# HGRN scores on four column strips, one input block on ScalarE's queue, a norm weight on GpSimd, and new figures for the planner

## The chip, the cores and the metric

The kernel runs on one core of a Trainium2 chip, as one program in one launch. The metric is device time in microseconds (us), from the first instruction to the end of the last, and a program's time is the median of its runs. The core's engines are TensorE (PE; its weight loads PEld), VectorE (DVE), ScalarE (ACT), GpSimd (POOL) and SyncE (SP), which here only issues transfers (DMAs). Each engine works through a queue of its own in order, and they wait for one another by semaphores. SBUF is the working memory; PSUM holds what PE writes.

## What is computed

One layer over 512 frames of width 2048. All is float32.

```python
proj = einsum('btd,dc->btc', x, w_in)              # 2048 -> 8320 columns
rw   = token_shift(proj[..., :4224])               # y + mu * (y one frame earlier - y)
r, k, v, z, wd, ad = split(rw)
# RWKV-7, 16 heads of 64: a gated recurrence over frames
kk = k * k_k;  kk = kk / max(norm(kk per head), 1e-12)
S_t = S_(t-1) * decay_t + (S_(t-1) a_t) b_t + v_t k_t;   o_t = S_t r_t
o_rwkv = (group_norm(o) + sum(r * k * r_k) * v) * silu(z)
# HGRN2, 8 heads of 128: gated linear recurrence, over chunks of 64 frames
att[t, s] = sum_d q[t, d] exp(b[t, d] - b[s, d]) k[s, d]   for s <= t
o_hgrn = rms_norm(att i + state part) * g_norm_w * silu(z)
y   = concat(o_rwkv, o_hgrn) @ w_out
out = layer_norm(ALPHA * x + y) * ln_w + ln_b
```

## The kernel before

*The main stream.* Nearly all of PE's work is the two projections. Each float32 operand is split in a high part of type fp32r (`xh`, `wh`) and the rest (`xl`, `wl`), and `three` (L485) issues high x high, high x low and low x high: three main matmuls of 128x128 by 128x512 for one block. Weights arrive in 512 KB tiles `wr` (two of them), on SP's queue, and each half tile is a *part*: `split` takes its high part on ScalarE (`wh`, L361) and the rest on VectorE (`wl`, L371). A part feeds 12 main matmuls. The input units come in a fixed order (`_order`), k, r, v, z for a pair of RWKV heads, then q, f, i, g for the HGRN heads; results are taken out of PSUM by queued evacuations (`shift`, `silu2`, `gates`: L362 on ScalarE, then L380 on VectorE).

*The planner.* Everything else is written as generators of `Op`s, which wait in queues: `preps` (`rwkv_prep`), `turns` (`rwkv_turn`), `groups`, `scans`, `heads` (`hgrn_heads`), `ends` (`hgrn_out`) and more. After each main matmul `plan.pump()` looks at the head of every queue and issues what it thinks can start. It keeps a clock for each engine, and each `Op` has a price in us for each engine that could do it; where there are two (`copy`: ScalarE or VectorE) the one that ends earlier is taken. A PE instruction is put in only when its operands, by these clocks, are nearly there. So the prices issue nothing, but they set the order of the instructions on all five engines. On the chip the engines follow that order and wait where it was too early. `SETS` lists in which function tables of ScalarE a function is found; the planner adds 1.3 to an `Op` whose table isn't the one it thinks loaded. The table loads themselves (ACT_TABLE_LOAD) are put in later, where the order needs them.

*What the steps of the prediction touch.*
- `turned` transposes a tile in 32x32 blocks on VectorE (`dtr`, L390), writes it to DRAM (`far<-q` for the `bk` tile of an RWKV pair, `far<-ksq` for others) and loads it back by rows (`q<-far`, four loads), all on SP's queue (L327). It tells the planner when the loads will have landed: 4.0 after the issue.
- `rwkv_prep` makes head norms: squares, `head_sums` (VectorE adds two halves, ScalarE takes the high part, VectorE the rest, into `ksq`), a product with a block of ones on PE (`mix<-ksq,ones_r`, L348), then Ln and Exp on ScalarE. `rwkv_turn` calls `turned` for `bk`, copies the turned tile on ScalarE (`q<-q`, 128x1024), and makes a second product with `ones_r`. So there are 8 copies and 16 such products.
- `hgrn_heads` builds a head's 128x128 score blocks from products of blocks of 32, 64 and smaller, of two heads at a time. At width 64 it makes both the scores between neighbours of 32 (`w1` = 32) and of 64 (`w1` = 64) in one bank of PSUM, and copies them into the block-diagonal tiles `dgs`. A product is placed in PSUM at a partition offset `g`: products with another offset stand on another strip of PE's columns.
- `fetch` loads the 16 input blocks `head[k]` (512 columns of x and three weight blocks). Block 0 comes in three pieces, one on ScalarE's queue; blocks 1 to 15 come whole, on SP's. `arrive` splits them. Before the first product PE runs nine products of zeros (L1225); the first three units are made by `product` (L1275).
- `row_last` and `finish_last` make the last 128 rows' last 512 columns, in two halves: add, statistics (L1632), the layer norm's mean and reciprocal root (`spread`, with the root on GpSimd, L403), products with the norm's weight (`less_mean`, `weigh`), two products on PE that bring the bias in (`made`), and the last four multiply-adds and stores.

## Time and profile before

| | |
|---|---|
| median of 3 runs | 1031.55 us (1031.42 to 1031.56) |
| the profiled execution's own time | 1033.02 us |
| its span, first instruction to last | 1031.2 us |
| PE busy | 1020.1 us, 99% |
| DVE, ACT, POOL busy | 789.9, 478.4, 42.6 us |
| granted clock | 1.00 |
| DMA | 130.82 MB, 127 GB/s in the mean |

A profile's page gives the busy time of each engine, the chain of work that ended last, and groups of equal instructions with their count, mean duration and the idle time before them. A timeline row has the start and the duration in us, engine, line, operation, out<-in tiles, shapes and a count; in brackets stands how long the engine had been idle and what released it. Main matmuls overlap in the pipeline: a row shows about 0.39 us for one, but their starts are what counts. A float32 product that isn't fp32r leaves two records. Lines are those of the kernel before.

### The profile page before, as it was taken

What the parts mean: (1) busy time and instruction counts of PE and PEld (TensorE: products, weight loads), DVE (VectorE), ACT (ScalarE), POOL (GpSimd) and SP (SyncE); (2) the same over time, 40 slices, a digit from 0 to 9 for tenths busy, and PEclk for the clock granted to TensorE, in tenths of its full rate; (3) what the DMA queues carried; (4) which work ended last, traced back from release to release, by engine and by line L of the source; (5) the groups of instructions that cost most, each with busy time, mean ns of one, the idle gap of its engine ahead of it and who ended that gap; (6) DMA issues with size and microseconds to landing.
All of it is one profiled execution on the core that took longest, in us unless ns stands there. A gap on an engine that the chain in (4) does not pass through costs nothing.

```text
span 1031.2 us, 19527 instructions
## 1 busy us (share of the span) xinstructions
PE 1020.1 (99%) x7636; PEld 843.2 (82%) x7636; DVE 789.9 (77%) x1687; ACT 478.4 (46%) x898; POOL 42.6 (4%) x77
## 2 busy tenths in 40 slices
PE   9999999999999999999999999999999999999997
PEld 8888878888878888888887888887888888888885
DVE  7477997679779988698998758887998888526556
ACT  6457344545363356464534554636435544323321
POOL 0000001001000010020000100100001010000000
PEclk9999999999999999999999999999999999999999
DMA  9134442233635322345353243253432256435613
GB/s 337 53 104 127 138 125 88 78 103 113 183 105 157 122 73 81 92 138 183 105 152 105 82 114 118 92 172 111 147 106 81 63 175 226 149 117 172 200 55 133
DMA packets 58700, 130.82 MB, mean 127 GB/s; under 512 B 9840, under 2 KB 25712, under 8 KB 58480
## 3 DMA queue, kind: packets, MB, share of 16 engines
q1 hardware_dynamic: 58464, 129.37, 39.7%
q8 instruction: 60, 0.98, 0.4%
q14 instruction: 32, 0.26, 0.1%
q10 hardware_dynamic: 144, 0.20, 0.1%
HBM read 111.06 MB, written 18.48 MB: 126 GB/s over the span
## 4 chain that ended last, share of the span: by engine, by line
PE 94%; DMA 2%; DVE 2%; ACT 1%; issue 1%; SPq 0%; DVEq 0%; ACTq 0%
PE main L485 71%; PE mix L348 9%; PE mix L485 8%; PE main L1275 3%; PE main L348 2%; DMA q<-far 1%; DMA far<-q 1%; PE mix L1225 0%; DVE inv L380 0%; SPq L327 0%; DVE wl L371 0%; DVE big L371 0%; DVE q L413 0%; DVE big L390 0%; ACT wh L361 0%
## 5 line engine op out<-in xcount | busy, mean ns | idle before, releaser
L485 PE MATMUL main<-xh,wl 128*128 128x512 f32 x864 | 340.0, 393 | 0.0
L485 PE MATMUL main<-xh,wh 128*128 128x512 f32 x864 | 339.5, 393 | 0.0
L485 PE MATMUL main<-xl,wh 128*128 128x512 f32 x864 | 339.0, 392 | 0.0
L361 ACT ACTIVATE wh<-wr 128x512 fp32r<-128x512 f32 x299 | 185.7, 626 | 194.4 <-PE main L485 139.0
L371 DVE TENSOR_TENSOR wl<-wr,wh 128x512 fp32r<-128x512 f32 x299 | 203.6, 682 | 56.0 <-ACT wh L361 53.9
L485 PEld LDWEIGHTS main<-xh,wh 128*128 128x128 f32 x864 | 162.4, 188 | 33.1
L485 PEld LDWEIGHTS main<-xh,wl 128*128 128x128 f32 x864 | 162.3, 188 | 33.1
L485 PEld LDWEIGHTS main<-xl,wh 128*128 128x128 f32 x864 | 162.3, 188 | 33.0
L485 PE MATMUL main<-wh,xl 128*128 128x512 f32 (+1 forms) x262 | 102.4, 391 | 0.0
L485 PE MATMUL main<-wh,xh 128*128 128x512 f32 (+1 forms) x262 | 101.8, 389 | 0.5 <-ACT t L362 0.5
L485 PE MATMUL main<-wl,xh 128*128 128x512 f32 (+1 forms) x262 | 101.9, 389 | 0.0
L485 PEld LDWEIGHTS main<-wh,xh 128*128 128x128 f32 x262 | 49.2, 188 | 10.8 <-ACT t L362 1.0
L485 PEld LDWEIGHTS main<-wh,xl 128*128 128x128 f32 x262 | 49.2, 188 | 10.0
L485 PEld LDWEIGHTS main<-wl,xh 128*128 128x128 f32 x262 | 49.2, 188 | 9.9
L362 ACT ACTIVATE t<-main,om 128x512 f32<-128x512 f32 x33 | 22.3, 686 | 51.9 <-PE main L485 42.6
L380 DVE SCALAR_TENSOR_TENSOR bd<-mix,pc,bd 64x64 f32<-64x64 f32 x112 | 31.7, 283 | 11.6 <-PE mix L348 7.8
L371 DVE TENSOR_TENSOR inv<-inv,inv 64x30 f32<-64x30 f32 (+14 forms) x120 | 38.5, 321 | 2.7
L371 DVE TENSOR_TENSOR inv<-inv 64x30 f32<-64x30 f32 (+14 forms) x120 | 38.5, 321 | 2.5
L380 DVE SCALAR_TENSOR_TENSOR t<-main,pr,t 128x511 f32<-128x511 f32 x33 | 24.3, 745 | 19.6 <-ACT t L362 19.5
L361 ACT ACTIVATE t<-mix 64x128 f32<-64x128 f32 (+2 forms) x66 | 18.0, 276 | 44.3 <-DVE zz L371 23.5
L371 DVE TENSOR_TENSOR t<-t,tot 128x256 f32<-128x256 f32 x96 | 37.2, 418 | 0.2
L362 ACT ACTIVATE t<-main 128x512 f32<-128x512 f32 x32 | 18.6, 593 | 28.7 <-PE main L485 28.6
(228 smaller groups left out, 1408.1 us busy)
## 6 DMA issues: line engine op xcount, KB each, us to landing
wr<-w_all SPq DMA_DIRECT2D x156, 512.0 KB, 3.6
q<-head SPq DMA_DIRECT2D x15, 448.0 KB, 5.8
far<-ksq SPq DMA_DIRECT2D x22, 256.0 KB, 3.2
far<-q SPq DMA_DIRECT2D x8, 512.0 KB, 5.0
q<-far SPq DMA_DIRECT2D x32, 128.0 KB, 4.4
g<-x_r SPq DMA_DIRECT2D x16, 256.0 KB, 4.0
t<-far SPq DMA_DIRECT2D x56, 64.0 KB, 3.5
spill<-g SPq DMA_DIRECT2D x12, 256.0 KB, 2.8
```

Of the source, the lines that this page charges most:

```text
L348: return Op([("pe", cost, lambda: pe.matmul(o, l, r, start=start, stop=stop, **kw))], [l, r], [o], mode="narrow" if narrow else "main" if ...
L361: return "act", cost, lambda: sc_e.activation(o, i, f, scale=scale)
L362: return "act", cost, lambda: sc_e.activation(o, i, f, scale=scale, bias=bias)
L371: return dve_op([a, b], o, lambda: dve.tensor_tensor(o, a, b, f), base=0.16 if o.shape[0] < P and size(o) == C and o.tensor.name in tags e ...
L380: return dve_op([a, b], o, lambda: dve.scalar_tensor_tensor(o, a, s, b, f1, f2), per=0.00113, base=0.085 if o.shape[0] == P else 0.25 if s ...
L485: pe.matmul(ps, l, r, start=first and i == 0, stop=last and i == 2)
L1275: pe.matmul(pss[a], *ops, start=k == 0 and low == of == 0, stop=k == KT - 1 and low == 1)
```

## The change

`hgrn_heads` puts the products of blocks of 32 on four strips of partitions in turn, where they stood on two, and copies them out in four pieces a head, where there were two. `fetch` issues block 1 on ScalarE's queue. In the last half row the multiply with the norm's weight goes to GpSimd, and is issued ahead of the statistics' root; it no longer stands in `finish_last`. The other edits change the planner's figures: Exp is found in its own table alone; `turned` tells 4.2, and 5.2 for 128x1024, as the time to landing; `tensor_scalar` and `copy` on VectorE are priced by whether they read PSUM; small `scalar_tensor_tensor`s, and transposes of 128 partitions, have new prices. `head_sums` passes a base price of 0.15.

```diff
--- before.py
+++ after.py
@@ -57,7 +57,7 @@
     return o + [(2, 14), (2, 15), (3, 13), (3, 14), (3, 15)]
 
 
-SETS = {AF.Sigmoid: ("sigmoid",), AF.Tanh: ("exp", "sigmoid"), AF.Exp: ("exp", "ln"), AF.Ln: ("ln",)}
+SETS = {AF.Sigmoid: ("sigmoid",), AF.Tanh: ("exp", "sigmoid"), AF.Exp: ("exp",), AF.Ln: ("ln",)}
 
 
 class Plan:
@@ -367,18 +367,23 @@
     def dve_op(reads, o, f, n=None, per=0.00104, base=0.07):
         return Op([("dve", base + (n or size(o)) * per, f)], reads, [o])
 
-    def tt(o, a, b, f=ALU.mult):
+    def tt(o, a, b, f=ALU.mult, base=None):
         return dve_op([a, b], o, lambda: dve.tensor_tensor(o, a, b, f),
-                      base=0.16 if o.shape[0] < P and size(o) == C and o.tensor.name in tags else 0.07)
+                      base=base or 0.16 if o.shape[0] < P and size(o) == C and o.tensor.name in tags else 0.07)
+
+    def banked(ap):
+
+        return 0.00104 if ap.tensor.name in plan.banks else 0.00076
 
     def ts(o, a, s1, s2, f1, f2=None):
         if f2 is None:
-            return dve_op([a], o, lambda: dve.tensor_scalar(o, a, s1, None, f1), per=0.0008)
-        return dve_op([a], o, lambda: dve.tensor_scalar(o, a, s1, s2, f1, f2), per=0.0008)
+            return dve_op([a], o, lambda: dve.tensor_scalar(o, a, s1, None, f1), per=banked(a))
+        return dve_op([a], o, lambda: dve.tensor_scalar(o, a, s1, s2, f1, f2), per=banked(a))
 
     def stt(o, a, s, b, f1, f2):
         return dve_op([a, b], o, lambda: dve.scalar_tensor_tensor(o, a, s, b, f1, f2), per=0.00113,
-                      base=0.085 if o.shape[0] == P else 0.25 if size(o) == C else 0.165)
+                      base=0.085 if o.shape[0] == P and size(o) > P else 0.12 if o.shape[0] == P
+                      else 0.21 if size(o) == C else 0.165)
 
     def red(o, i):
         return dve_op([i], o, lambda: dve.tensor_reduce(o, i, AX.X, ALU.add), size(i))
@@ -387,6 +392,8 @@
         return dve_op([i], o, lambda: dve.copy_predicated(o, m, i))
 
     def dtr(o, i):
+        if i.shape[0] == P:
+            return dve_op([i], o, lambda: dve.transpose(o, i), per=0.0011, base=0.05)
         return dve_op([i], o, lambda: dve.transpose(o, i), per=0.0019)
 
     def dve_tt_way(o, a, b, f=ALU.mult):
@@ -411,7 +418,7 @@
             f = lambda: dve.tensor_scalar(o, i, scale, None, ALU.mult)
         else:
             f = lambda: dve.tensor_copy(o, i)
-        return Op([act_way(o, i, AF.Copy, scale), ("dve", 0.075 + size(o) * 0.00105 + moved(o, i), f)], [i], [o])
+        return Op([act_way(o, i, AF.Copy, scale), ("dve", 0.07 + size(o) * banked(i) + moved(o, i), f)], [i], [o])
 
     def blocks(t, n):
 
@@ -424,11 +431,12 @@
         yield lambda: by_now(tmp)
         yield lambda: plan.clock["sp"] <= plan.clock["pe"] + 0.2
         send(far, tmp.rearrange("p b c j -> p b (c j)"))
-        there = plan.busy[tmp.tensor.name] = (plan.clock["sp"] + 4.0, "dma")
+        late = 4.2 + max(0, size(tmp) - T) * 0.002
+        there = plan.busy[tmp.tensor.name] = (plan.clock["sp"] + late, "dma")
         for b in range(rows):
             yield lambda: there[0] <= plan.clock["pe"] and plan.clock["sp"] <= plan.clock["pe"] + 0.2
             send(dst(b).rearrange("i a c j -> i a (c j)"), far[:, b].rearrange("(a i) x -> i a x", a=4))
-        plan.ready[dst(0).tensor.name] = (plan.clock["sp"] + 4.0, "dma")
+        plan.ready[dst(0).tensor.name] = (plan.clock["sp"] + late, "dma")
 
 
 
@@ -671,7 +679,7 @@
         own = slice(0, 64)
         yield tt(f[own], f[own], g[own], ALU.add)
         yield act(hl[own], f[own], AF.Copy)
-        yield tt(hl[64:128], f[own], hl[own].bitcast(F32), ALU.subtract)
+        yield tt(hl[64:128], f[own], hl[own].bitcast(F32), ALU.subtract, 0.15)
 
     def rwkv_prep(S, p):
         if p == 0:
@@ -1096,19 +1104,20 @@
                     for i, (q, k) in enumerate(zip(q1, k1)):
                         pi = ps[:, P * (2 * v + i) : P * (2 * v + i) + P]
                         for b in range(4 * n):
-                            c, o = b // n, b * 2 * w1
-                            g = b % 2 * 64
-                            at = (b // 2 if w1 == 64 else c) * w1
+                            o = b * 2 * w1
+                            g, at = (b % 2 * 64, b // 2 * 64) if w1 == 64 else (b % 4 * 32, b // 4 * 32)
                             yield mm(pi[g : g + w1, at : at + w1], k[:, o : o + w1], q[:, o + w1 : o + 2 * w1])
                 for v, (w1, k1, q1) in enumerate(both):
                     for i, dg in enumerate(dgs):
                         pi = ps[:, P * (2 * v + i) : P * (2 * v + i) + P]
-                        for g in range(2):
-                            part = pi[64 * g : 64 * g + w1].rearrange("p (c t) -> p c t", t=w1)
-                            if w1 == 64:
-                                yield copy(dg[:64, g::2, 64:], part)
-                            else:
-                                yield copy(dg[64 * g : 64 * g + 32, :, 64 * g + 32 : 64 * g + 64], part)
+                        if w1 == 64:
+                            for g in range(2):
+                                yield copy(dg[:64, g::2, 64:], pi[64 * g : 64 * g + 64].rearrange("p (c t) -> p c t", t=64))
+                        else:
+                            for b in range(4):
+                                c, g = b // 2, b % 2 * 64
+                                yield copy(dg[g : g + 32, c::2, g + 32 : g + 64],
+                                           pi[32 * b : 32 * b + 32, :64].rearrange("p (c t) -> p c t", t=32))
             drop(ps)
             if w == 64:
                 drop(*fs)
@@ -1230,7 +1239,9 @@
 
     def fetch(k):
         raw = firsts[k] = take("q4", [P, T + FIRST * P])
-        if k:
+        if k == 1:
+            nc.scalar.dma_start(raw, head[k])
+        elif k:
             send(raw, head[k])
         else:
 
@@ -1467,7 +1478,7 @@
                 y, y, AF.Identity, scale=rs, bias=mv[:, 3:4]))], [], []), k + k_r + k_m, k)
             done.add(f"scaled{t}_{d}")
 
-    def finish_last(t, pbs, weigh):
+    def finish_last(t, pbs):
 
 
         mv, rs = take("mv", [P, 4]), take("rs", [P, 1])
@@ -1487,7 +1498,6 @@
         def norm():
             yield small(ts(mv[:, 2:3], mv[:, 0:1], -1.0, None, ALU.mult), k_mv, k_n)
             yield less_mean(0)
-            yield from weigh()
             yield small(stt(mv[:, 3:4], mv[:, 0:1], -1.0, rs, ALU.mult, ALU.mult), k_mv + k_r, k_m)
             yield keyed(Op([("act", 0.25, lambda: sc_e.activation(dg, ident, AF.Copy, scale=mv[:, 3:4]))], [], []),
                         k_m, [dg.tensor.name])
@@ -1623,19 +1633,21 @@
                 kc = y_keys(t, d * T + c.start, d * T + c.stop)
                 yc, pc = y[:, c], halves[i]
 
-                def weigh():
+                def weigh(way=tt):
                     w = lnw[0][:, 0, d * T + c.start : d * T + c.stop]
-                    yield keyed(tt(yc, yc, w), kc, kc)
+                    yield keyed(way(yc, yc, w), kc, kc)
 
                 yield keyed(tt(yc, yc, pc, ALU.add), kc + [pc.tensor.name], kc)
                 yield keyed(Op([("dve", 0.07 + T // 2 * 0.00105,
                                  lambda: dve.bn_stats(stats[:, t, d + i], yc))], [], []), kc, [f"stat{t}"])
                 if i == 1:
+                    yield from weigh(lambda o, a, b: pool_tt(o, a, b, ALU.mult))
+                if i == 1:
 
                     yield room(mix=2)
                     pbs = {e: take("mix") for e in (2, 3)}
                     plan.add(scans[1], biased(pbs))
-                    yield from finish_last(t, pbs, weigh)
+                    yield from finish_last(t, pbs)
                     return
                 yield from weigh()
```

All prices feed one order, and the whole order after the start differs. Both programs have 21 table loads and the same matmuls. VectorE has 1719 instructions where it had 1689, ScalarE 887 where it had 901 (transfers included). Three places follow.

ScalarE, second head pair: from the weight split (`wh`) whose low part stands just behind the transpose of `bk` on VectorE, to the copy of the turned tile. Before:

```order
L361 ACTIVATE wh_1167<-wr_1072 128x512
L362 ACTIVATE t_1182<-main_1083 128x512
L361 ACTIVATE wh_1193<-wr_1124 128x512
L361 ACTIVATE wh_1214<-wr_1124 128x512
L361 ACTIVATE wh_1241<-wr_1174 128x512
L361 ACTIVATE wh_1263<-wr_1174 128x512
L361 ACTIVATE q_1157<-q_757 128x1024
L362 ACTIVATE t_1282<-main_1180 128x512
```

and now:

```order
L361 ACTIVATE wh_1119<-wr_1003 128x512
L361 ACTIVATE wh_1142<-wr_1080 128x512
L361 ACTIVATE wh_1165<-wr_1080 128x512
L362 ACTIVATE t_1182<-main_1082 128x512
L361 ACTIVATE wh_1193<-wr_1128 128x512
L361 ACTIVATE wh_1217<-wr_1128 128x512
L361 ACTIVATE wh_1240<-wr_1170 128x512
L361 ACTIVATE q_1110<-q_770 128x1024
L361 ACTIVATE ksq_1252<-t_741 32x512 x2
```

Behind the first row, four splits stood ahead of the copy, and now five. Counted so over the eight pairs, it was 4, 4, 4, 4, 5, 5, 4, 4 and is 5, 5, 5, 5, 6, 5, 4, 5.

SP, sixth pair: the tile's way out (`far<-q`) and back (`q<-far`) among the weight loads. Before:

```order
L327 DMA wr_5606<-w_all 128x1024
L327 DMA far_5586<-q_5585 128x1024
L327 DMA q_5099<-far_5586 32x4x256
L327 DMA wr_5652<-w_all 128x1024
L327 DMA q_5099<-far_5586 32x4x256 x3
L327 DMA wr_5702<-w_all 128x1024
```

and now:

```order
L327 DMA wr_5605<-w_all 128x1024
L327 DMA far_5584<-q_5583 128x1024
L327 DMA wr_5649<-w_all 128x1024
L327 DMA q_5207<-far_5584 32x4x256 x4
L327 DMA wr_5699<-w_all 128x1024
L327 DMA wr_5755<-w_all 128x1024
```

The weight load that stood behind the first of the four loads stands ahead of all four. At the seventh pair a spill of another tile stood among the four, and now stands ahead of them.

ScalarE, fourth pair: Ln and Exp of the head norms (`ksq<-ksq`), with the table loads ahead of each, and the evacuation `t_3106`, whose second step on VectorE follows. Before:

```order
L361 ACTIVATE ksq_3061<-t_2682 32x512 x2
L361 ACTIVATE wh_3068<-wr_3002 128x512
L362 ACT_TABLE_LOAD
L362 ACTIVATE ksq_3079<-ksq_3079 128x512
L361 ACTIVATE wh_3091<-wr_3002 128x512
L362 ACT_TABLE_LOAD
L362 ACTIVATE ksq_3079<-ksq_3079 128x512
L362 ACTIVATE t_3106<-main_3009,om 128x512
L362 ACTIVATE pf_2986<-t_2906 128x8x64
```

and now:

```order
L361 ACTIVATE ksq_3065<-t_2679 32x512 x2
L361 ACTIVATE wh_3072<-wr_3006 128x512
L362 ACT_TABLE_LOAD
L362 ACTIVATE ksq_3084<-ksq_3084 128x512
L361 ACTIVATE wh_3095<-wr_3006 128x512
L362 ACTIVATE t_3106<-main_3013,om 128x512
L362 ACT_TABLE_LOAD
L362 ACTIVATE ksq_3084<-ksq_3084 128x512
L361 ACTIVATE wh_3118<-wr_3057 128x512
L362 ACTIVATE pf_2980<-t_2910 128x8x64
```

The evacuation of `main` stood behind the second table load and Exp, and now stands ahead of both.

## The prediction

> **What bounds the kernel now.** I read the page's busy shares first, then its chain of work, then PE's own timeline for the places where two matmul starts stand further apart than they must.
>
> ```profile
> PE 1020.1 (99%) x7636; PEld 843.2 (82%) x7636; DVE 789.9 (77%) x1687; ACT 478.4 (46%) x898; POOL 42.6 (4%) x77
> PE 94%; DMA 2%; DVE 2%; ACT 1%; issue 1%; SPq 0%; DVEq 0%; ACTq 0%
> 890.11 43.52 PE mix L485 x192
> ```
>
> The first two rows are the page's busy time and chain, the third a piece of the chain in order of time. PE is the bound nearly everywhere. In the undisturbed piece 192 main matmuls take 43.52 us, so one costs 0.227 us from start to start. The kernel has 3876 of these with 512 columns, so most of the span can't move. What can move is narrow matmuls, the two ends, and places where PE waits. A start that comes more than 0.227 us after the one before it shows a wait:
>
> ```profile
> 134.34 0.39 PE L485 MATMUL main<-wh,xl 128*128 128x512 f32 x1
> 135.28 0.50 PE L485 MATMUL main<-wh,xh 128*128 128x512 f32 x1 [0.55 <-ACT t L362]
> ...
> 300.81 0.39 PE L485 MATMUL main<-xl,wh 128*128 128x512 f32 x1
> 302.00 0.47 PE L348 MATMUL mix<-ksq,ones_r 128*128 128x512 f32 x1 [0.80 <-ACT wh L361]
> ...
> 546.08 0.39 PE L485 MATMUL main<-xh,wl 128*128 128x512 f32 x1
> 548.00 0.50 PE L348 MATMUL mix<-ksq,ones_r 128*128 128x512 f32 x1 [1.53 <-DVE ksq L371]
> ...
> 700.28 0.39 PE L485 MATMUL main<-xl,wh 128*128 128x512 f32 x1
> 701.35 0.47 PE L348 MATMUL mix<-ksq,ones_r 128*128 128x512 f32 x1 [0.68 <-DVE ksq L371]
> ...
> 748.20 0.39 PE L485 MATMUL main<-xl,wh 128*128 128x512 f32 x1
> 748.63 0.47 PE L348 MATMUL mix<-ksq,ones_r 128*128 128x512 f32 x1
> ```
>
> These are pairs from PE's timeline. Less 0.227 each, the waits are 0.71, 0.96, 1.69, 0.84 and 0.20 us: 4.4 us together. Four of the five are a head-sum product (ones_r) that stands in PE's order before its operand is there. Nothing else in the middle of the program waits as long. The largest, followed back, is this piece of the chain:
>
> ```profile
> 536.12 5.96 DMA q<-far
> ...
> 542.19 1.06 ACT q L361
> ...
> 545.89 0.69 DVE wl L371
> ...
> 547.26 0.70 DVE ksq L371
> ...
> 548.00 0.50 PE mix L348
> ```
>
> ```profile
> ACT q L361 <- DMA q<-far: 15.7, 5, 3.5
> q<-far SPq DMA_DIRECT2D x32, 128.0 KB, 4.4
> ```
>
> A block that went through DRAM to be turned lands late (5.96 us after the last of its four loads was issued, where 4.4 is the median). ScalarE stands at its copy of it and all behind it is late: evacuations, weight splits, and then the head sums on VectorE. The row of waits says that five of the eight such copies waited, 15.7 us in all and 3.5 at most. The waits of PE at 135, 548, 701 and 749 follow four of them: 3.44 us. The fifth, at 302, has another cause:
>
> ```profile
> 291.13 1.28 ACT L362 ACT_TABLE_LOAD   x1 [0.60 <-DVE ksq L376]
> ...
> 293.59 1.28 ACT L362 ACT_TABLE_LOAD   x1
> ...
> 296.13 0.75 DVE L380 SCALAR_TENSOR_TENSOR t<-main,pr,t 128x511 f32<-128x511 f32 x1 [1.83 <-ACT t L362]
> ...
> 301.17 0.69 DVE L371 TENSOR_TENSOR ksq<-t,ksq 64x512 fp32r<-64x512 f32 x1
> ```
>
> ScalarE loads a table before Ln and another before Exp, 1.28 us each. The planner before charges nothing for the second, since its list lets Exp run in Ln's table. VectorE then idles 1.83 us for an evacuation behind that load, and its head sum at 301.17 is late.
>
> **The planner's figures.** They issue no instruction; they move the order. *The turned blocks.* The planned landing goes from 4.0 to 5.2 us for the 128x1024 blocks and to 4.2 for 128x512; the measured median of 4.4 lies between. In the order shown above, ScalarE has one more weight split between the transpose's weight part and the copy at six of the eight places; a split serves 12 main matmuls, 12 x 0.227 = 2.7 us of PE. Counted in the program as written out, the main matmuls between VectorE's transpose and the copy go from 65, 58, 62, 58, 80, 60, 60, 58 to 73, 65, 69, 71, 84, 64, 64, 71. The worst two places, sixth and seventh, gain only four (0.9 us). But there the head-sum product also moves away from the copy, from 29 to 37 and from 17 to 25 main matmuls (1.8 us), and the four loads leave SP together, no longer with a weight load or a spill among them. 0.9 + 1.8 = 2.7 us against waits of 1.69 and 0.84. So of 3.44 us I keep 0.5 and take 2.9 away (bounds: 0 and 3.44). *The table.* With the second load priced, the evacuation is put ahead of it: 1.28 us earlier against a wait of 0.96. I take 0.85 (bounds 0 and 0.96). *What is late next.* Every place in the middle is ordered anew, and a cheaper price (the transposes, copies out of SBUF) lets the planner put consumers closer. The old order has five waits in 24 such places (16 head sums, 8 copies); I allow the new one a middle-sized one, 0.9 us (bounds 0 and the old 4.4). The base of 0.15 in `head_sums` does nothing: `base or 0.16 if ... else 0.07` gives 0.07 for a 512-wide row whatever base is.
>
> **Four strips.** Sixteen products of 32 columns in each of four groups change from two column strips to four; no instruction is added on PE, and 16 more small evacuations stand on ScalarE and VectorE, long before the block of scores is multiplied.
>
> ```profile
> 187.59 0.70 PE L348 MATMUL mix<-t 128*32 128x32 f32 x32
> ...
> 145.74 0.89 PE L348 MATMUL mix<-q,t 128*32 128x48 f32 x64
> ...
> 166.38 0.76 PE L348 MATMUL mix<-t,t 128*32 128x16 f32 x63
> ...
> L348 PE MATMUL mix<-t x32: 196/196/217, 187.6 to 188.1; 128*32 128x32 f32 x32
> ```
>
> A product leaves two records. Less the last one's own 0.2 us, two strips take 0.50 / 16 = 31 ns a product; four strips take 0.69 / 32 = 22 ns at 48 columns and 0.56 / 31.5 = 18 ns at 16. 32 columns lie between: 20 ns. 16 x 11 ns x 4 groups = 0.7 us (bounds 0.6 and 0.85, or 0 if the strips don't matter). The Trainium skill's page "TensorE: Matmul & The Clock Gate", Part 1 ("Wait — 56ns, not 53.3ns?"), speaks against this: starts never come closer than about 25 ns however few the columns. By that rule the strips bring nothing and the sum ends at 1028.5. The rows have records 9 to 16 ns apart, so I go by them.
>
> **The last norm weight.** On VectorE it is one multiply in a chain that ends the program:
>
> ```profile
> 1021.69 0.43 DVE L1632 BATCH_NORM_STATS2 stats<-inv 128x6 f32<-128x256 f32 x1
> ...
> 1022.71 0.55 POOL L403 TENSOR_TENSOR rs<-mv,mhalf 128x1 f32<-128x1 f32 x1 [10.02 <-DVE mv L376]
> 1022.72 0.75 DVE L380 SCALAR_TENSOR_TENSOR inv<-big,mv,inv 128x512 f32<-128x512 f32 x1
> 1023.39 0.42 DVE L371 TENSOR_TENSOR inv<-inv,big 128x256 f32<-128x256 f32 x1
> 1023.73 0.15 DVE L380 SCALAR_TENSOR_TENSOR mv<-mv,rs 128x1 f32<-128x1 f32 x1
> ```
>
> ```profile
> L406 POOL MEMSET t<- 128x512 f32 x8 | 4.1, 535 | 0.0
> L403 POOL TENSOR_TENSOR sm<-sm,mhalf 128x8 f32<-128x8 f32 x8 | 16.0, 1998 | 144.2 <-DVE sm L377 144.2
> ```
>
> Gone from VectorE, it would let the bias (1023.73) start at 1023.48: 0.25 us. But GpSimd gets it ahead of the reciprocal root, which the bias waits for, and whose work can start at 1022.71. The multiply can start at about 1022.2. GpSimd's price for it isn't in the trace: below it lies a memset's half row, about 0.3 us, above it the 2.0 us of a power on 8 columns. It is nearest to the memset, with two operands to read: 0.7. Then the root runs 1022.9 to 1023.45 and 0.2 us is gained. At 0.3 us it is 0.25; at 2.0 the root ends at 1024.75 and about 1.0 is lost. The Trainium skill's "GPSIMD Engine Reference", Section 4.1, says to leave elementwise products to VectorE, since GpSimd takes about twice as long; twice the 0.42 above is an estimate of 0.84, which would leave 0.1 us of gain.
>
> **Block 1 on ScalarE's queue.**
>
> ```profile
> 6.20 0.63 ACT L361 ACTIVATE xh<-q 128x512 fp32r<-128x512 f32 x1 [1.39 <-DMA q<-head]
> ...
> 7.80 0.84 PE L1275 MATMUL main<-xh,t 128*128 128x512 f32 x3
> ```
>
> Block 1 is split from 6.20 on and PE wants it at 7.80: it is hidden, and earlier landing brings 0. One more issue on ScalarE ends long before its first activation. It could delay block 0's halves by sharing the engines, at most by that slack of 1 us; I take 0, with 0.3 against it in the range.
>
> **The sum.** The profiled execution took 1033.02 us with a span of 1031.2, so 1.8 lies around the span; the runs' median is 1031.55, and since the terms are differences I set them against it: -2.9 - 0.85 + 0.9 - 0.7 - 0.2 + 0 = -3.75, so 1027.8 us.
>
> **Rivals.** *The waits come back elsewhere.* The price of each wait is an accident of the order, and the order is new in every stage; for it speaks that 12 of 16 head sums met next to no wait before, and which four did doesn't follow from the old figures alone. New waits of the old 4.4 us leave the strips and the tail: 1031.55 - 0.7 - 0.2 = 1030.7. *The head-sum price does nothing, and those products go on waiting.* Only the evacuation's 0.71 goes: 1031.55 - 0.71 - 0.7 - 0.2 = 1029.9. Against it: 0.70 at 547.26 against a planned 0.60 explains 0.1 us of lateness, not 1.69. *VectorE becomes the bound*, the one that ends slower:
>
> ```profile
> 500.00:525.00 25.00, 25.00 (x135) 20.63 (x133) 24.16 (x48) 9.32 (x15) 0.16 (x1) 1.00 0.36 109
> L413 DVE COPY inv<-big 64x512 f32<-64x512 f32 x4 | 1.7, 418 | 0.1
> ```
>
> In that stretch VectorE is busy 24.16 of 25 us. The new order gives it 30 more instructions, moved from ScalarE since a copy out of SBUF is priced lower; at 0.42 us for the widest, at most 12.5 us. If they land where it is full, weight splits and head sums run late. With the four gains above the waits must exceed 4.65 + 2.06 = 6.7 us for the kernel to be slower; six of the longest seen, 6 x 1.69 = 10.1, would give 1026.9 + 10.1 = 1037.0. Against it: its mean load is 77%, and the moved copies are spread over the program.
>
> **How the numbers follow.** A change of 0.2% (2.06 us) is what a measurement tells from none: faster is below 1029.5, slower above 1033.6. The forecast has 0.60, its own range 1026.3 (all waits gone, no new one) to 1029.4. Waits that come back: 0.20. Head sums that go on waiting: 0.08. VectorE: 0.10. The last 0.02 lies below the forecast's range. So faster 0.62, same 0.28, slower 0.10. The range 1026.3 to 1031.0 leaves out VectorE's case and the upper part of the first rival.
>
> **What would show it.** On ScalarE, the copies after the transpose wait less than 15.7 us in sum, and PE's starts before an ones_r product stand 0.23 apart. The 32-column group of 32 records takes 0.52 us, not 0.70. GpSimd's multiply starts near 1022.2 in the old time and ends before 1023; a bias held by the root shows as a wait on POOL. The first main matmul still starts at 4.9. I am wrong if ScalarE's waits go and PE's don't, if PE waits on a weight split (wl) in the stretches where VectorE is over 23 of 25, or if new waits sum to 4 us.

## The result, and the profile after

The changed kernel takes 1027.97 us, the median of 6 runs (1027.53 to 1028.74). The kernel before, run beside it, took 1031.55 us (6 runs, 1030.06 to 1031.98). The ratio is 0.9967, with a 95% interval of 0.9955 to 0.9979: 3.4 us faster, with 2.2 to 4.6 in the interval. Predicted were 1027.8 us and faster.

The profiled execution of the changed kernel took 1027.53 us with a span of 1025.6. That of the kernel before took 1033.02, which is 1.5 us above its median; the changed one's is 0.4 below its own. So the two traces differ by 5.6 us of span where the medians differ by 3.6, and a comparison of the traces overstates the move.

Busy times and chain of the changed kernel, from the page:

```profile
PE 1017.4 (99%) x7636; PEld 842.4 (82%) x7636; DVE 792.7 (77%) x1717; ACT 471.7 (46%) x883; POOL 41.1 (4%) x78
PE 96%; DVE 2%; issue 1%; DMA 0%; ACT 0%; POOLq 0%; POOL 0%; DVEq 0%; SPq 0%; ACTq 0%
```

The chain held 2% of DMA and 1% of ScalarE before. Both are gone, and PE has 96% of it where it had 94%. VectorE has 2.8 us more work and ScalarE 6.7 us less: the copies moved as foreseen. Of the waits of PE and of the turned blocks, these rows are left:

```profile
PE mix L348 <- ACT ksq L1502: 1.7, 1, 1.7
ACT q L361 <- DMA q<-far: 1.1, 2, 0.8
PE mix L1234 <- DVE inv L1232: 1.0, 1, 1.0
PE mix L348 <- DVE zz L371: 0.3, 1, 0.3
PE mix L348 <- issue: 0.2, 1, 0.2
```

ScalarE waits 1.1 us for turned blocks where it waited 15.7. The rows with L1502 and L1234 are the program's end and its start, as before. PE's rows for an evacuation, a weight split and the head sums (`ksq L371`, 2.2 us) have gone. In PE's timeline three of the places of the prediction look so now:

```profile
300.13 0.39 PE L493 MATMUL main<-xl,wh 128*128 128x512 f32 x1
300.36 0.43 PE L348 MATMUL mix<-ksq,ones_r 128*128 128x512 f32 x1
...
548.03 0.40 PE L493 MATMUL main<-wh,xh 128*128 128x512 f32 x1
548.26 0.40 PE L348 MATMUL mix<-ksq,ones_r 128*128 128x512 f32 x1
...
699.27 0.40 PE L493 MATMUL main<-xl,wh 128*128 128x512 f32 x1
699.51 0.40 PE L348 MATMUL mix<-ksq,ones_r 128*128 128x512 f32 x1
```

Each head-sum product starts 0.23 us after the main matmul ahead of it. They stood 1.19, 1.92 and 1.07 apart.

**Where the time went.** PE's span can be split so that nothing is left over: the time to the first main matmul; 893.60 us for the wide matmuls (512 columns at 0.227, 256 at 0.119 from start to start, the same in every kernel here); what these take above that, with waits over 0.15 us listed apart (*waits* from 12 us on, *slow starts* before that, where matmuls stand about 0.43 apart; e4's 0.19 and e9's 0.40 in that column are a wait for block 1 instead); the groups of narrow matmuls, with the waits inside them and directly before them; and the last part, from the first bias product of the last half row to the end. All of it is worked out from the starts in PE's own timeline. e1 to e12 are the runs of the next section.

| kernel | first main | wide, above 893.60 | of it waits | of it slow starts | narrow groups | last part | span |
|---|---|---|---|---|---|---|---|
| before | 4.92 | 17.96 | 4.41 | 0.74 | 104.55 | 10.21 | 1031.24 |
| changed | 5.07 | 12.26 | 0 | 0 | 104.28 | 10.41 | 1025.62 |
| e1 figures only | 4.91 | 13.74 | 0.66 | 0.95 | 104.86 | 10.30 | 1027.42 |
| e2 changed, old figures | 5.97 | 20.82 | 6.09 | 1.73 | 103.86 | 10.57 | 1034.83 |
| e3 root first | 5.67 | 12.29 | 0 | 0 | 104.35 | 10.44 | 1026.36 |
| e4 block 1 on SP | 4.88 | 12.84 | 0 | 0.19 | 103.99 | 10.48 | 1025.79 |
| e5 strips only | 4.92 | 19.89 | 6.44 | 0.17 | 104.10 | 10.24 | 1032.75 |
| e6 Exp's table only | 5.01 | 16.00 | 3.21 | 0.77 | 109.46 | 10.22 | 1034.30 |
| e7 landing only | 4.91 | 15.47 | 2.43 | 0.74 | 104.44 | 10.21 | 1028.64 |
| e8 VectorE's prices only | 4.92 | 19.41 | 5.03 | 0.95 | 103.86 | 10.26 | 1032.05 |
| e9 figures and strips | 4.91 | 13.60 | 0.48 | 0.40 | 104.10 | 10.31 | 1026.52 |
| e10 as e9, base 0.15 working | 4.91 | 13.09 | 0 | 0.74 | 103.73 | 10.26 | 1025.60 |
| e11 first half's weight on GpSimd | 5.49 | 12.47 | 0 | 0.34 | 104.11 | 10.27 | 1025.95 |
| e12 changed, again | 6.40 | 14.67 | 0.58 | 1.69 | 103.97 | 10.45 | 1029.10 |

From before to changed: start +0.15, wide -5.70 (waits -4.41, slow starts -0.74, the rest -0.55), narrow -0.27, end +0.20; together -5.62. The slow starts belong to the execution and not to the change: changed and e12 are the same program, and show 0 and 1.69. Since before's trace was a slow execution of its kernel, every difference to its row makes a gain look about 1.5 us too large, or a loss too small.

### The profile page after: what moved, and what is told of

It is laid out like the page before. It is cut to its first block, busy times and chain, and to the rows that moved or that the text cites. A ratio compares the mean times of both kernels' runs of the same rounds, so it can differ in the third digit from the quotient of the medians.

```text
span 1025.6 us, 19514 instructions
## 1 busy us (share of the span) xinstructions
PE 1017.4 (99%) x7636; PEld 842.4 (82%) x7636; DVE 792.7 (77%) x1717; ACT 471.7 (46%) x883; POOL 41.1 (4%) x78
## 4 chain that ended last, share of the span: by engine, by line
PE 96%; DVE 2%; issue 1%; DMA 0%; ACT 0%; POOLq 0%; POOL 0%; DVEq 0%; SPq 0%; ACTq 0%
PE main L493 73%; PE mix L348 9%; PE mix L493 8%; PE main L1286 3%; PE main L348 2%; DMA t<-spill 0%; PE mix L1234 0%; DVE wl L371 0%; DVE inv L384 0%; DVE q L420 0%; DVE big L397 0%; DVE t L371 0%; PE mix L352 0%; DVE inv L371 0%; POOLq L1758 0%
## 5 line engine op out<-in xcount | busy, mean ns | idle before, releaser
L371 DVE TENSOR_TENSOR wl<-wr,wh 128x512 fp32r<-128x512 f32 x299 | 203.6, 682 | 64.2 <-ACT wh L361 59.3
L371 DVE TENSOR_TENSOR inv<-inv,inv 64x30 f32<-64x30 f32 (+14 forms) x120 | 38.4, 320 | 2.5
L371 DVE TENSOR_TENSOR inv<-inv 64x30 f32<-64x30 f32 (+14 forms) x120 | 38.4, 320 | 2.5
L371 DVE TENSOR_TENSOR t<-t,tot 128x256 f32<-128x256 f32 x96 | 37.2, 416 | 0.2
```

What stands on the lines that cost most here:

```text
L371: return dve_op([a, b], o, lambda: dve.tensor_tensor(o, a, b, f), base=base or 0.16 if o.shape[0] < P and size(o) == C and o.tensor.name i ...
```

## The experiments

**e1 and e2: the figures, and everything but the figures.** e1 is the kernel before with the planner's figures of the change; e2 is the changed kernel with the old figures.

```diff
 e1, on before:
-SETS = {... AF.Exp: ("exp", "ln"), ...}
+SETS = {... AF.Exp: ("exp",), ...}
-        there = ... (plan.clock["sp"] + 4.0, "dma")
+        late = 4.2 + max(0, size(tmp) - T) * 0.002
+        there = ... (plan.clock["sp"] + late, "dma")
+    and banked(), ts, stt, dtr, copy as in the change
 e2, on the changed kernel: the same lines the other way round
```

> The kernel before with all of the planner's new figures, and nothing else of the change. Theory (the figures remove PE's waits): no pair of main matmul starts in the middle of the program stands more than 0.15 us too far apart, or such waits sum to under 0.5 us, where before had 4.4; the group of 32 records of 32 columns keeps its 0.70 us; from the first bias product to the end of the span it is 10.2 us as before. 1031.55 - 4.4 + 0.4 = 1027.6 for what the figures bring alone, 1027.5 to 1028.9. Rival (a wait's place and size are an accident of whatever order comes out): another order has waits of 2 to 5 us, 1029 to 1032.

> The changed kernel with all of the planner's figures put back to those of before; strips, block 1 on ScalarE's queue and the norm weight on GpSimd stay. Theory: the waits are back, 3 to 5 us in sum, most of them behind copies of turned blocks (over 10 us of ScalarE waiting on q<-far) and behind a second table load; only the strips are gained, about 0.9 us in four groups: 1030.6, 1029.8 to 1031.4. Rival (accident of the order): waits anywhere from 0.5 to 6 us, and ScalarE's waits on q<-far no guide to them.

e1: 1029.0 us (11 runs, 1028.6 to 1029.91), ratio 0.9981 [0.9972, 0.9989]. e2: 1035.1 us (1034.35 to 1036.61), ratio 1.0035 [1.0022, 1.0049]. e1 missed the range of its theory by 0.1 us (its waits are 0.66 us where under 0.5 were expected), e2 by nearly 4. The waits of e1, and then those of e2:

```profile
ACT q L361 <- DMA q<-far: 5.0, 3, 3.2
PE mix L348 <- DVE ksq L371: 0.5, 1, 0.5
```

```profile
ACT q L361 <- DMA q<-far: 16.6, 7, 4.2
PE mix L348 <- DVE ksq L371: 1.7, 2, 1.3
PE main L485 <- DVE t L380: 1.5, 1, 1.5
PE main L485 <- DVE wl L371: 1.4, 2, 1.2
PE main L1278 <- DVE xh L1262: 0.7, 1, 0.7
```

The figures alone take 2.0 us off. The three other edits alone add 3.6 us, though they shorten PE's narrow groups: under the old figures the new order has 6.1 us of waits in the middle where the order before had 4.4, behind seven turned blocks instead of five. Both together are 3.4 us faster, so the parts don't add: the figures are worth 2.0 us on the old kernel and 7.0 us on the changed one (3.6 + 3.4).

**e5: the strips alone.** The strips' lines of the change on the kernel before, nothing else.

```diff
-                            c, o = b // n, b * 2 * w1
-                            g = b % 2 * 64
-                            at = (b // 2 if w1 == 64 else c) * w1
+                            o = b * 2 * w1
+                            g, at = (b % 2 * 64, b // 2 * 64) if w1 == 64 else (b % 4 * 32, b // 4 * 32)
 ... and the four copies a head, as in the change
```

> The kernel before with the four strips (and their four copies) alone. What is asked of it: how much of the waits goes with the old figures, and how much with any new order. Theory (old figures make waits): 3 to 6 us of PE waits in the middle again, though at other places, and the four groups of 32 and 64 columns 0.22 to 0.24 us shorter each, 0.95 in all: 1029.5 to 1031.5. Rival (accident): the waits may be anything, and under 1.5 us would speak for it.

It took 1035.25 us (1033.8 to 1037.55), ratio 1.0035 [1.0022, 1.0048]: slower, a miss by nearly 4 us. The strips do what was said of them, as these rows of the changed kernel show (the first row's counterpart was 0.70):

```profile
192.66 0.46 PE L348 MATMUL mix<-t 128*32 128x32 f32 x32
193.05 0.69 PE L348 MATMUL mix<-t,t 128*64 128x64 f32 x16
193.66 0.60 PE L348 MATMUL mix<-zz,q 128*128 128x128 f32 x3
```

From 192.66 to the matmul behind the group it is 1.00 us; it was 1.24. But the 16 small evacuations that come with them shift every later decision of the planner, and under the old figures the shifted order waits 6.44 us, again mostly at turned blocks:

```profile
ACT q L361 <- DMA q<-far: 17.6, 7, 4.9
PE mix L348 <- DVE ksq L371: 2.5, 2, 1.4
```

The order of PE's matmuls in e5 is that of e2 from the first to the last, and so is ScalarE's order; their times (1035.25 and 1035.1 us) and waits (6.44 and 6.09) agree too. So what e2 loses, it loses by the order that comes with the strips, and not by the two moved instructions. It also shows that the waits of an order come back in another execution.

**e6, e7, e8: one group of figures each, on the kernel before.**

```diff
 e6: AF.Exp: ("exp",)          # Exp in its own table alone
 e7: late = 4.2 + max(0, size(tmp) - T) * 0.002
 e8: banked(), ts, stt, dtr, copy as in the change
```

> The kernel before with one figure new: Exp is found in its own table alone. Theory: the waits of a head sum behind two table loads go (about 1 us in before), those behind turned blocks stay, 2 to 4 us, with ScalarE's waits on q<-far above 10 us: 1030.0 to 1031.5. Rival (accident): no such split.

> The kernel before with one figure new: the planned landing of turned blocks, 4.2 and 5.2 us where it was 4.0. Theory: ScalarE's waits on q<-far fall from 15.7 us to under 6, PE's waits behind them (3.44 us in before) to under 1, and a wait of about 1 us behind the table loads stays: 1028.0 to 1030.0; the largest part of the gain that the figures bring is here. Rival: the VectorE prices matter more, and this one alone stays above 1030.3.

> The kernel before with the new VectorE prices alone (tensor_scalar, copy, scalar_tensor_tensor, transposes). Theory: they let the turned block go out 0.8 us sooner and its copy follow sooner too, so ScalarE's waits on q<-far stay above 10 us and PE waits 3 to 6 us: 1030.3 to 1032.5. Rival (VectorE's true prices are what lets the planner place head sums): waits under 1.5 us, below 1029.5.

e6: 1037.61 us (1035.67 to 1039.61), ratio 1.0057 [1.0036, 1.0078]. e7: 1030.13 us (1029.54 to 1030.68), ratio 0.9987 [0.9978, 0.9996]. e8: 1034.47 us (1033.29 to 1035.62), ratio 1.003 [1.002, 1.004]. e6 and e8 missed their figures by 6 and 2 us, e7 by 0.1. The waits of e6, e7 and e8, in this order:

```profile
ACT q L361 <- DMA q<-far: 7.7, 3, 3.4
PE mix L352 <- DVE t L371: 2.3, 1, 2.3
PE main L485 <- DVE t L380: 1.0, 1, 1.0
PE mix L348 <- DVE ksq L371: 1.0, 1, 1.0
```

```profile
PE mix L348 <- DVE ksq L371: 1.5, 2, 1.2
PE main L486 <- DVE t L380: 0.4, 1, 0.4
```

```profile
ACT q L361 <- DMA q<-far: 11.4, 5, 3.4
PE mix L348 <- DVE ksq L371: 3.5, 6, 1.4
```

The landing time (e7) is the only figure that helps alone: no row of ScalarE waiting for a turned block is left, and the waits fall by 2.0 us in the traces; the medians gain 0.8. With the new prices on VectorE but the old landing time (e8) the copies ahead of the head sums still wait (11.4 us), and six of the products do: the prices probably put the sums closer to their products, which no row shows by itself. Exp's table alone (e6) removes the wait at 302 and gets new ones in the narrow groups (109.46 us against 104.55), the longest at a transpose on PE.

**e3 and e11: why the end got longer.** In e3 GpSimd takes the reciprocal root first and the multiply behind it; in e11 GpSimd multiplies the first half row, about 1.4 us earlier, and VectorE the second.

```diff
 e3:
-                    yield from weigh(lambda o, a, b: pool_tt(o, a, b, ALU.mult))
 (in finish_last)
         yield from spread(t, mv, rs, 5)
+        yield from weigh()          # on GpSimd
 e11:
-                    yield from weigh(lambda o, a, b: pool_tt(o, a, b, ALU.mult))   # second half
 ...
-                yield from weigh()
+                yield from weigh(lambda o, a, b: pool_tt(o, a, b, ALU.mult))   # first half
 (in finish_last)
             yield less_mean(0)
+            yield from weigh()          # second half, on VectorE
```

> The changed kernel with the reciprocal root issued on GpSimd ahead of the last norm weight, where it stood behind. In the changed kernel the root took 0.99 us behind the multiply (0.55 before) and the bias waited for it. Theory (GpSimd pays some 0.4 us when it goes from one kind of operation to the next at once): the root takes 0.55 again and starts with the mean, the bias starts 0.45 us earlier, and the last stretch, from the first bias product to the span's end, is 9.9 to 10.0 us in place of 10.41 (10.21 before); the multiply, now second, takes about 1.1. Rival (VectorE's wide multiply-add at the same time slows GpSimd): the root keeps about 0.9 to 1.0 us, and the stretch is 10.3 to 10.5.

> The changed kernel with the first half row's weight on GpSimd and the second half's on VectorE, so that GpSimd's multiply ends about 1 us before its root starts. If a root is slow because the multiply stands directly ahead of it or still runs beside it, it takes 0.55 us again and the last part 10.2 us. If GpSimd pays for the change of operation, the root takes 0.9 to 1.0 us and holds the bias as in the changed kernel: last part 10.4 us.

e3 took 1028.28 us and e11 1027.84, one run each, so the end is read from the traces. e3's theory failed: the root takes 0.55 again, but the last part is 10.44 us, not 9.9 to 10.0. The changed kernel, then e3, then e11:

```profile
1016.42 0.73 POOL L403 TENSOR_TENSOR inv<-inv,big 128x256 f32<-128x256 f32 x1 [9.56 <-PE mix L348]
...
1016.90 0.80 DVE L384 SCALAR_TENSOR_TENSOR inv<-big,mv,inv 128x512 f32<-128x512 f32 x1
1017.10 0.99 POOL L410 TENSOR_TENSOR rs<-mv,mhalf 128x1 f32<-128x1 f32 x1
1018.13 0.16 DVE L384 SCALAR_TENSOR_TENSOR mv<-mv,rs 128x1 f32<-128x1 f32 x1 [0.44 <-POOL rs L410]
```

```profile
1017.60 0.55 POOL L410 TENSOR_TENSOR rs<-mv,mhalf 128x1 f32<-128x1 f32 x1 [10.01 <-DVE mv L380]
...
1018.11 0.84 POOL L403 TENSOR_TENSOR inv<-inv,big 128x256 f32<-128x256 f32 x1
1018.28 0.68 DVE L384 SCALAR_TENSOR_TENSOR mv<-mv,rs 128x1 f32<-128x1 f32 x1
```

```profile
1015.47 0.73 POOL L403 TENSOR_TENSOR inv<-inv,big 128x256 f32<-128x256 f32 x1 [8.13 <-issue]
1017.36 0.55 POOL L410 TENSOR_TENSOR rs<-mv,mhalf 128x1 f32<-128x1 f32 x1 [1.16 <-DVE mv L380]
...
1018.37 0.15 DVE L384 SCALAR_TENSOR_TENSOR mv<-mv,rs 128x1 f32<-128x1 f32 x1
```

The multiply costs 0.73 us on GpSimd. Directly behind it the root takes 0.99 us instead of 0.55, and VectorE waits 0.44 us for it with the bias. With the root first it takes 0.55, but then VectorE's small bias instruction, which runs beside the multiply, takes 0.68 us instead of 0.15. With 1.16 us between multiply and root, the root takes 0.55 and the last part 10.27 us. So a change of operation on GpSimd doesn't in itself make the root slow. VectorE's wide instruction beside it isn't enough either: before, in e3 and in e11 it runs beside the root, which takes 0.55. But there the root starts 0.01 us ahead of it, while in the four traces with a root of 0.99 (changed, e2, e4, e12) the wide instruction had started 0.20 to 0.30 us earlier. Whether the root is slow because it follows the multiply directly, or because VectorE was already at work, isn't settled; a run with the multiply directly ahead of the root and VectorE idle wasn't made.

**e4 and e12: block 1's queue.** e4 is the changed kernel with block 1 on SP's queue; e12 is the changed kernel itself once more.

```diff
-        if k == 1:
-            nc.scalar.dma_start(raw, head[k])
-        elif k:
+        if k:
             send(raw, head[k])
```

> The changed kernel with block 1 loaded from SP's queue again. Main theory: the first main matmuls at half clock (0.75 us of excess in the profile before, 0.08 in the one after) come from when the clock opens in that execution, not from the queue; the first main matmul starts at 4.9 to 5.1 in both, the middle and the end stay as in the changed kernel, and the excess over 0.227 us of the first nine starts is anything from 0 to 0.8. Rival (block 1's queue matters): the first main matmul starts 0.15 us earlier than 5.07 and the start of block 1's products moves by the same, with the excess of 0.75 us back.

> The changed kernel again, beside e9 and e10 on the same chip, so that a difference of half a microsecond can be read: 1027.5 to 1028.7 us as before. My theory puts it 0.35 to 0.8 us above e9; if the two moved instructions cost nothing that a median shows, the two agree within 0.2 us.

e4 took 1027.68 us in its one run; e12 1028.32 us (10 runs, 1027.58 to 1031.01), ratio 0.9971 [0.9962, 0.998]. VectorE's first split of block 0 and PE's first main matmul, in the changed kernel and then in e12's profiled execution, which was the slowest of its ten:

```profile
4.63 0.29 DVE L1270 CAST xh<-q 128x256 fp32r<-128x256 f32 x1 [3.63 <-DMA q<-head]
5.07 1.62 PE L1286 MATMUL main<-xh,t 128*128 128x512 f32 x6
```

```profile
5.96 0.29 DVE L1270 CAST xh<-q 128x256 fp32r<-128x256 f32 x1 [4.97 <-DMA q<-head]
6.40 2.90 PE L1286 MATMUL main<-xh,t 128*128 128x512 f32 x6 [1.14 <-DVE xh L1270]
```

The split waits for the second half of block 0's x, on SP's queue. In all nine traces with block 1 on SP's queue it starts at 4.1 to 4.4 us, and the first main matmul at 4.88 to 5.01. In the five with block 1 on ScalarE's it starts at 4.63 to 5.96, and the first main matmul at 5.07, 5.49, 5.67, 5.97 and 6.40. The loads themselves, from issue to landing (median), before and then e12:

```profile
q<-head SPq DMA_DIRECT2D x2, 128.0 KB, 3.1
q<-head ACTq DMA_DIRECT2D x1, 192.0 KB, 3.2
```

```profile
q<-head ACTq DMA_DIRECT2D x1, 448.0 KB, 5.2
q<-head SPq DMA_DIRECT2D x2, 128.0 KB, 4.0
```

Block 0's halves take 4.0 us where they took 3.1 (3.2 in the changed kernel's trace): block 1, issued at 1.17 us on the other queue, runs beside them. So the edit delays what PE wants first. In e4 the first main matmul starts 0.19 us before 5.07, as the rival had it; the slow starts that it expected back didn't come.

It also brings something, which the prediction took as nothing. ScalarE's split of block 1 and the first product with it in e9, whose block 1 is on SP's queue, and then the split in the changed kernel:

```profile
6.79 0.63 ACT L361 ACTIVATE xh<-q 128x512 fp32r<-128x512 f32 x1 [2.06 <-DMA q<-head]
7.47 0.96 PE L1284 MATMUL main<-xh,t 128*128 128x512 f32 x3 [0.24 <-ACT xh L361]
```

```profile
5.33 0.63 ACT L361 ACTIVATE xh<-q 128x512 fp32r<-128x512 f32 x1 [0.65 <-DMA q<-head]
```

e9's product starts 0.40 us late (e4's 0.19); the changed kernel's, at 7.22, doesn't wait. In before this didn't show: block 1's split began at 6.20, and the slow starts had moved its first product to 7.80. What is left in the end differs from execution to execution: the 46th main matmul starts at 15.3 to 15.8 us in e4, e5 and e9 (SP's queue, one slow start at most), at 15.4, 16.0 and 16.1 in the changed kernel, e3 and e11 (ScalarE's), and at 18.1 and 18.3 in e2 and e12 (ScalarE's too), of which 1.7 are slow starts. Whether a late first matmul brings on more slow starts isn't shown.

**e9 and e10: what is left when the two costs are taken out.** e9 is the kernel before with all figures and the strips: block 1 on SP's queue, the last norm weight on VectorE. e10 adds the brackets without which `head_sums`' base price is lost.

```diff
 e10, on e9:
-    base=base or 0.16 if o.shape[0] < P and size(o) == C and o.tensor.name in tags else 0.07)
+    base=base or (0.16 if o.shape[0] < P and size(o) == C and o.tensor.name in tags else 0.07))
```

> Before plus all planner figures plus the four strips; block 1 stays on SP's queue and the last norm weight on VectorE. My theory: the figures and the strips carry the gain, the two moved instructions cost 0.15 us or more at the start and 0.2 us at the end. So this kernel is 0.35 to 0.8 us faster than the changed one: 1027.2 us (1026.7 to 1027.7), PE's waits in the middle at most 1.5 us, first main matmul at 4.9 us, 10.2 us from the first bias product to the end. Rival, the moved instructions pay through the order that follows them: the waits come back (4 us or more) and the time is 1029.5 us or more.

> As e9, with the brackets that let the base price of 0.15 in head_sums take effect (0.68 us for that subtraction where the planner had 0.60 and the traces have 0.70). Theory that the order has reached a floor where all real prices are in: PE's waits stay at 1.5 us or less, the time is within 0.5 us of e9 (1026.7 to 1027.7). Rival, that each new order draws its waits anew: they lie between 2 and 7 us and the time between 1028.5 and 1033.

e9: 1027.07 us (5 runs, 1026.6 to 1028.24), ratio 0.9959 [0.9946, 0.9971], as expected. Beside it e12 took 1028.32, 1.25 us more where I had written 0.35 to 0.8: e9 is the fastest kernel here, and four of its five runs are below the fastest of e12's ten. Its start (4.91) and end (10.31) are near the old ones. PE's order in the middle is the changed kernel's, so the moved instructions pay nothing through the order, against the rival. The one wait there, 0.48 us, is for a weight load that took 6.10 us (3.5 is the median); e12 waits 0.58 at the same place, and the changed kernel's trace doesn't. By the ratios e9 is about 2.3 us better than e1, give or take 1.6; it differs from e1 by the strips alone, which shorten PE's groups by 0.96, and by the order that comes with them. Whether that order brings the rest isn't shown. e10: 1027.99 us (1027.49 to 1029.16), ratio 0.997 [0.9957, 0.9982]. Its order differs from e9's from 245 to 864 us, and no wide matmul waits there, so this new order drew no new waits. But it is no faster than e9, and 0.3 us above what I had written. Why it is 0.9 us above e9 the table doesn't tell: e10's trace is of its fastest execution, e9's of its slowest. Its row of turned blocks is worth a look:

```profile
ACT q L361 <- DMA q<-far: 7.6, 4, 3.4
```

ScalarE waits 7.6 us and no wide matmul of PE does, so a wait of ScalarE need not reach PE. That the work between copy and head sum covers it is likely, but not shown.

## Why the prediction was right, and where it wasn't

*Waits behind turned blocks and the second table load: right, and more.* I kept 0.5 + 0.11 us of the five waits; none is left in the trace. What I allowed for new ones, 0.9 us, was about what came, and it lies inside narrow groups. These are only 0.27 us shorter, though the strips shorten them by 0.96, so some 0.7 us is new there; PE's idle time inside them is 0.65 us where it was 0.17 (the row on `zz` is one of these waits). The net of these terms was put at -2.85 us; the traces show -4.41 + 0.7 = -3.7. Since before's trace is of an execution 1.5 us above the median, part of that excess is the execution's own.

*The rival of the accidental order: wrong here, right next door.* I gave 0.20 to waits that come back, arguing that an order is new at every place. Orders under all new figures that differ in the middle (e1, changed, e10) wait 0 to 0.66 us there. The two orders under old figures (before; e2 and e5) wait 4.4 to 6.4, under one group of new ones (e6, e7, e8) 2.4 to 5.0. So in these eight orders the sum of the waits follows the figures, all of them together; which places they hit looks like an accident. What I had not seen is that the other edits, with the old figures, would have made the kernel slower (e2, and e5 with the strips alone): the figures pay for the strips too.

*VectorE as the bound: no.* It is busy 792.7 us, 77% as before, with 30 instructions more, and PE's rows name it for 0.3 us in the middle.

*The strips: mechanism right, term too small.* I took 20 ns a product and 0.7 us. The row gives (0.46 - 0.20) / 16 = 16 ns, and four groups 4 x 0.24 = 0.96 us, beyond my bound of 0.85. The value lies below the 18 ns of the 16-column products, which I had taken as the lower end. By the Trainium skill's rule that I weighed ("TensorE: Matmul & The Clock Gate", Part 1), that starts never come closer than about 25 ns, nothing would have come; the 16 products stand 16 ns apart, their 32 records 8, so on column strips that rule doesn't hold here.

*The last norm weight: the sign was wrong.* The step "then the root runs 1022.9 to 1023.45" failed: the multiply's price was right (0.73 us against my 0.7), but I carried the root's 0.55 over from a row where GpSimd had been idle. It took 0.99. Instead of -0.2 us it is +0.20 (10.21 to 10.41). What I had named as the sign of it, a bias that waits on POOL, is the row at 1018.13. The Trainium skill's "GPSIMD Engine Reference", Section 4.1, gave twice VectorE's time, an estimate of 0.84 for the multiply; it took 1.7 times 0.42.

*Block 1: hidden as a landing, not as a load.* I named the sharing of the engines and its bound, "at most by that slack of 1 us", but took 0. The edit moves the first main matmul by 0.15 us in the changed kernel's trace and by up to 1.5 (6.40) in e12's. The slack that I had used belongs to block 1's consumer, while the loads that are delayed are block 0's, which have none. And the 7.80 at which PE wanted block 1 was read from an execution with slow starts: at full rate it wants it at about 7.1. Block 1's split, which starts anywhere from 5.5 to 7.0 us with SP's queue and takes 0.63, can then come too late (e4, e9).

*The base of 0.15:* `base or 0.16 if ...` does give 0.07, as read from the code; e10, where it works, gains nothing.

So the forecast of 1027.8 met 1027.97 partly by luck, because errors of both signs cancel: waits and strips brought more, start and end cost what I had put at a gain or nothing.

## What to carry to other kernels

Where prices set an order, correct them together: here each group changed alone, but for the landing time, made the kernel slower, and an edit that shortens the bounding engine's work was lost under stale prices. An instruction's duration is read from a row with the same neighbours, on its own engine and on the one beside it, above all for an engine that was idle before. A transfer moved to a second queue is charged to the transfers that run beside it, not only to who waits for it.

## What the runs showed of the hardware

*The first matmuls' rate differs between executions of one kernel.* Main matmuls at the start stand 0.43 us apart instead of 0.23, for none of them in the changed kernel's trace and for eight in e12's, the same program. The six matmuls in the row at 6.40 above take 2.90 us; those at 5.07 take 1.62. The Trainium skill's page "TensorE: Matmul & The Clock Gate", Part 1 ("The HAM clock gate"), says that PE runs at half rate for about the first 3.4 us of work and that the number of slow matmuls varies from run to run. The traces agree that the number varies, from none to eight, with up to 1.7 us lost. They don't agree on the 3.4 us: PE had been at work on the products of zeros since 1.05 us, without a break in before, where the slow starts last until about 6.3 us, and with a break of 1.14 us in e12, where they last until 9.5. The profile's clock reads 1.00 in these stretches all the same, so there the half rate is seen in the distances alone. The same rate comes back in e6 when PE had idled 2.31 us in the middle of the program:

```profile
876.81 0.98 PE L352 MATMUL mix<-cst,t 128*128 128x128 f32 x4 [2.31 <-DVE t L371]
877.44 0.77 PE L485 MATMUL main<-wh,xh 128*128 128x512 f32 x1
878.01 0.63 PE L485 MATMUL main<-wl,xh 128*128 128x512 f32 x1
878.44 0.63 PE L485 MATMUL main<-wh,xl 128*128 128x512 f32 x1
```

A 128x512 matmul takes 0.63 us there instead of 0.39, and their starts stand 0.43 apart until 879.7; the granted clock is 0.55 in the mean from 876.6 to 879.7 us, and 1.00 before. So this wait cost about 0.9 us beyond itself (it stands in the table among e6's waits). Waits of up to 1.5 us, as in the kernel before, e2 and e5, didn't do this.

*Instructions beside or directly behind a multiply on GpSimd take longer.* Directly behind a 128x256 multiply on GpSimd a root of 0.55 us takes 0.99, with VectorE at work beside it. Beside such a multiply a VectorE instruction of 0.15 us takes 0.68, and one of 0.75 takes 0.80 (0.89 in e2).
